# Hymba layer on one Trainium2 core: Toeplitz taps from on-chip tiles, bias tiles built on chip in two halves, and broadcast columns turned by transposes

## The chip, the cores and the metric

One core of a Trainium2 chip runs the whole layer as one launch. The metric is the device time in microseconds (us). The kernel before takes 2327.94 us, the median of three runs (2321.54 to 2329.34 us).

## The reference, cut to what matters

One encoder layer over 2048 frames of width 1024, in float32. One projection gives a state-space input `u` (512 columns: 32 groups of 16) and the queries, keys and values of 8 attention heads of width 64. Both halves are normalised, concatenated, projected and added to the residual; a SwiGLU feed-forward part and a last norm follow.

```python
h = rmsnorm(x, norm_mix_g[l]);  proj = h @ w_in[l]
# state space, per group of 16 channels, 64 complex states
bu = jnp.einsum('bsgh,gph->bsgp', uf, b_bar)
_, states = lax.associative_scan(combine, (a, bu), axis=1)
y = jnp.einsum('bsgp,ghp->bsgh', states, c_mat).real + d_skip * uf
# attention: own 64-frame chunk and the 8 before it
rel = jnp.arange(BAND)[None, :] - LEFT_CHUNKS * CHUNK - jnp.arange(CHUNK)[:, None]
bias = rel_bias[:, jnp.clip(rel, -MAX_REL, MAX_REL) + MAX_REL]
scores = einsum('bnqhd,bnkhd->bhnqk', qc, kb) / math.sqrt(HEAD_DIM) + bias
x = x + concat(rmsnorm(y_ssm), rmsnorm(y_att)) @ w_out[l]
x = x + (silu(h2 @ w_gate[l]) * (h2 @ w_up[l])) @ w_down[l]
```

The bias depends on the distance between query and key alone, so that each row of a bias tile is a window, one element further on, of one row of numbers. The state-space layer is computed in blocks of L = 8 frames: a small Toeplitz matrix of 16x16 taps C·A^k·B (plus D on the diagonal) inside a block, and a scan over blocks.

## The kernel before, in words

Nearly every matmul is split into three (`mm3`, L146): each float32 operand is a rounded part (`hi`) and a rest (`lo`), and hi·hi, hi·lo and lo·hi are added in PSUM. TensorE takes them in program order; a scheduler with priorities has laid the instructions out, and each engine runs its own list in order.

**u phase (`u_phase`).** The 2048 frames are four blocks of 512, in the order 1, 2, 3, 0 (`BLOCKS`). For a block, `prep` loads eight tiles of the transposed input (`xt`, L440, 256 KB each) and four tiles of the input itself (`w<-in_x`, L449, 512 KB each), both issued by SyncE (SP). ScalarE (ACT) makes `hi` from each `xt` (L442) and VectorE (DVE) `lo` (L443); ACT squares the `x` tiles and sums them (L450), and `newton` makes the reciprocal root of four columns on DVE (L104 to L112). A `group` is one 128-row slice of `u`: 24 matmuls into one PSUM bank. `finish` (called after the first group of the next block) spreads the four columns of roots over a 128x512 tile (`spread`, L122, bank `pp`), which ACT copies (`pb`, `rsn`), and DVE multiplies each group by it (`us`), which GpSimd (POOL) writes to DRAM. The `pp` banks are two (`psum2`).

**Prologue of the state space (`ssm_prologue`, a generator).** It advances in steps at places that `u_phase` chooses: `LONG = 1, 3, 2` steps after the first group of the later blocks. DVE makes the scaled inputs `bbr`, `bbi` (the B matrix), the powers `pr`, `pi`, the outputs `v` (four tiles, one for four pairs of groups, DRAM copy `vs`) and the inputs `wt` (four). POOL then makes the high powers `a8` and `sw`. The taps come from reloaded copies: `bbr`, `bbi` go to DRAM `bbs` by four POOL DMAs and come back as `bbg`, `vs` comes back as `vg` and `v`, with real and imaginary parts stacked on 128 partitions; then 32 matmuls of 128x16 weights and 128 columns (`pp<-vg,bbg`, `pp<-v,bbg`) and ACT copies into `kt`, which POOL writes to DRAM (`kts`). At the end `transposes` turns the 32 halves of `wt` for the DRAM tensor `bsts`.

**The first attention unit.** It makes the queries and keys of one pair of heads: two chains of 24 matmuls into the `pf` banks. The prologue's last steps are taken between its groups of six matmuls (`PRO`, L44). After it, copies on ACT and DVE and a DMA make `q2h`, `q2l` and `k2`, and the first scores (`sc`) follow.

**Attention and state space.** A score tile is one PSUM pair (`sc`); DVE adds the bias tile `nb` and takes the row minimum (`s`, L829), ACT takes the exponential, TensorE transposes the result (`pt`, L81), and another matmul with `v` follows (`pj`). The bias tiles of 128x640 are loaded per head, 32 times, from a DRAM table `nbms` (`load_nb`, L800). The table is filled in the u phase from the 768-wide rows `nbs`: one DMA of 1024x640 (2560 KB, DRAM to DRAM, L521) in front of the second prepared block's `xt` loads, and two that put 1e30 into the two corners that a frame may not see (L524). `pv_scale` (L880) spreads reciprocal sums over tiles. The state-space units load `U`, `Bst` (from `bsts`), `Tm` (from `kts`) and `Vm` through SP (L549 in `ssm_unit`) and run between heads, with their scan on POOL (L587 to L621).

**The rest.** Gate and w_out (bank `big`), the gate and up projections (`X`, `Y`) and the down projection (`ps`), which hold most of the time. `rstd_steps` (L141) spreads roots there too.

A spread is the same matmul everywhere: the weights are a column broadcast to 128x128, the moving operand is the identity.

Of the kernel before, what the change touches and what calls it, by code (L numbers as in the profile page):

```python
# [13 lines left out]
ALU = mybir.AluOpType  # L14
AX = mybir.AxisListType

P = 128
# [47 lines left out]
LONG = 1, 3, 2  # L65
# [56 lines left out]
def spread(k, te, pb, o, c):  # L122

    for i in range(4):
        te.matmul(pb[:, i * P : (i + 1) * P], o[:, c + i : c + i + 1].to_broadcast([P, P]), k.ident[:], start=True, stop=True)


def rstd_steps(k, te, psum, pool, tag, sq, n, out, **kw):

    nt = out.shape[-1] // P  # L130
    ps = k.t(psum, *tag, **kw)
    sqs = sq if isinstance(sq, list) else [sq]
    for i in range(nt):
        for m, sq in enumerate(sqs):
            te.matmul(ps[:, i : i + 1], sq[:, i * P : (i + 1) * P], k.ones[:], start=m == 0, stop=m == len(sqs) - 1)
    with k.tc.high_priority():
        o = newton(k, pool, ps[:, :nt], n, nt)
    yield
    pb = k.t(psum, *tag, **kw)
    for i in range(nt):  # L140
        te.matmul(pb[:, i * P : (i + 1) * P], o[:, i : i + 1].to_broadcast([P, P]), k.ident[:], start=True, stop=True)  # L141
    k.nc.scalar.copy(out, pb[:, : nt * P])
    yield
# [13 lines left out]
def ssm_prologue(k, ident, S):  # L157
# [3 lines left out]
    with tc.tile_pool(name="pro", bufs=1) as p:  # L161
# [126 lines left out]
        def transposes(b_, wt):  # L288
            bst = k.t(p, "v" if b_ > 1 else "vg", [P, 9 if b_ > 1 else 8, 2, NS], bufs=2)[:, :8]
# [42 lines left out]
        for g2 in range(2):  # L332
            for c, bt in ((0, bbr), (1, bbi)):
                nc.gpsimd.dma_start(S["bb"][:, g2, c].rearrange("q n m -> n q m"), bt[g2 * NS : (g2 + 1) * NS])
        yield
        wts = []
        for b_ in range(4):
            qs = slice(4 * b_, 4 * b_ + 4)
# [7 lines left out]
            yield  # L346
        for b_ in range(4):
# [3 lines left out]
            wts.append(wt)  # L351
            yield
# [13 lines left out]
        kt = k.t(p, "kt", [CH, 8, P], bufs=2)  # L366
        nc.gpsimd.memset(kt[:], 0.0)
        for b_ in range(4):
            nc.gpsimd.dma_start(S["kt"][:, 8 * b_ : 8 * b_ + 8, 0], kt[:])
        bb = k.t(p, "bbg", [P, NG, CH])  # L370
        nc.sync.dma_start(bb[:], S["bb"].rearrange("q g c n m -> (c n) (q g) m"))
        dm = k.t(p, "cm1", [P, 576])[:CH, : NG * CH].rearrange("c (g m) -> c g m", g=NG)
        V.tensor_tensor(dm, ident[:CH, :CH].unsqueeze(1).to_broadcast([CH, NG, CH]),
                        ddt[:].unsqueeze(2).to_broadcast([CH, NG, CH]), op=ALU.mult)
        vgs = []
        for b_ in range(4):
            vgs.append(k.t(p, "vg", [P, 8, P], bufs=2)[:] if b_ < 2 else k.t(p, "v", [P, 9, P], bufs=2)[:, :8])
            nc.sync.dma_start(vgs[b_], S["v"].rearrange("q g c n m -> (c n) (q g) m")[:, 8 * b_ : 8 * b_ + 8, :P])
        for b_ in range(4):
            gs = slice(8 * b_, 8 * b_ + 8)  # L380
            vg = vgs[b_]
            kt = k.t(p, "kt", [CH, 8, P], bufs=2) if b_ < 2 else k.t(p, ("bc", "small")[b_ - 2], [CH, 8, P])
            if b_ == 0:
                yield
            for g0 in (0, 4):
                ps = k.t(k.pro_psum, "pp", [P, 512])[:].rearrange("p (a b) -> p a b", a=4)
                for g in range(4):
                    k.te.matmul(ps[:CH, g, :], bb[:, 8 * b_ + g0 + g, :], vg[:, g0 + g, :], start=True, stop=True)
                nc.scalar.copy(kt[:, g0 : g0 + 4, :], ps[:CH])
                yield  # L390
            V.tensor_tensor(kt[:, :, :CH], kt[:, :, :CH], dm[:, gs], op=ALU.add)
            nc.gpsimd.dma_start(S["kt"][:, gs, 1], kt[:])
# [4 lines left out]
def u_phase(k, ident, S, aw):  # L397
# [3 lines left out]
    with ExitStack() as cx:  # L401
# [113 lines left out]
        for n in range(1, NSB):  # L515
            last, b = BLOCKS[n - 1 : n + 1]
            prep(b)
            if n == 1:
                corner = k.t(p1, "corner", [64, 64])
                nc.gpsimd.memset(corner[:], 1e30)  # L520
                nc.sync.dma_start(S["nbm"][:], bass.AP(S["nb"].tensor, S["nb"].offset + 1, [[768, H], [1, P], [1, 640]]))  # L521
            if n == 3:
                for m in range(2):
                    corners = nc.sync.dma_start(S["nbm"][:, m * 64 : m * 64 + 64, m * 576 : m * 576 + 64].rearrange("h p c -> p h c"), corner[:].unsqueeze(1).to_broadcast([64, H, 64]))  # L524
                    tc.keep_in_program_order(corners)
# [3 lines left out]
            long(LONG[n - 1])  # L529
            if n == NSB - 1:  # L530
                att = att_phase(k, ident, S, aw, X[b], lambda: ST[b])
                next(att)
                long(1)
            now += [group(b, f, f in pf) for f in (1, 2)]
# [3 lines left out]
        long(7 - sum(LONG))  # L538
    return pro, att

# [122 lines left out]
def att_phase(k, ident, S, aw, x0, roots):  # L663

    tc, nc, io, pfs = k.tc, k.nc, k.io, k.pfs
    with ExitStack() as cx:
# [129 lines left out]
        nbs = {}  # L796

        def load_nb(h):
            nb = k.t(aa, "nb", [P, 640], bufs=2)
            nc.sync.dma_start(nb[:], S["nbm"][h])  # L800
            return nb
# [72 lines left out]
        def pv_scale(st):  # L874
# [4 lines left out]
            for i in range(4):  # L879
                k.ta.matmul(pb[:, i * P : (i + 1) * P], rb[:, i].rearrange("p h d -> p (h d)"), ident[:], start=True, stop=True)  # L880
# [19 lines left out]
        aa = cx.enter_context(tc.tile_pool(name="aa", reuse_waits="tile", bufs=1))  # L900
        sp = tc.alloc_tile_pool(name="ssm", reuse_waits="tile", bufs=1)
# [670 lines left out]
def block_kernel(tc, io, phases="pusamf"):  # L1572
# [3 lines left out]
    with ExitStack() as cx:  # L1576
# [4 lines left out]
        def pp():  # L1581
# [5 lines left out]
            "k": k.t(dram, "ks", [2, H, P, SB]), "nbm": k.t(dram, "nbms", [H, P, 640]), "nb": k.t(dram, "nbs", [H, 768]),  # L1587
# [3 lines left out]
            "bb": k.t(dram, "bbs", [NPR, 2, 2, NS, CH]), "kt": k.t(dram, "kts", [CH, NG, 2, P]),  # L1591
# [17 lines left out]
        with tc.tile_pool(name="powers", bufs=1) as p:  # L1609
            S["a8"] = k.t(p, "a8", [P, 2, NPR, 16])  # L1610
            S["sw"] = k.t(p, "sw", [P, 3, 2, NPR])
            with tc.tile_pool(name="apf", bufs=2, space=bass.MemoryType.PSUM, reuse_waits="tile") as k.pfs:
# [64 lines left out]
```

## Time and profile before

| what | us |
|---|---|
| median of three runs | 2327.94 |
| the profiled execution | 2328.99 |
| its span, first to last instruction | 2327.2 |
| TensorE busy in the span | 2197.0 (94%) |
| u phase, to the first matmul of the attention unit | 0 to 116.8 |
| that unit, with taps | 116.8 to 135.4 |
| first score matmul | 143.24 |
| attention and state space | to about 760 |
| gate and w_out | 760 to 1010 |
| gate and up projections | 1010 to 1865 |
| down projection, last norm | 1865 to 2327 |

Times in the profile are counted from the first instruction of the span; 1.8 us of the profiled execution lie around it. PE is TensorE, SPq an instruction of SyncE that issues a DMA, and a row of the chain of waits reads: start, duration, what it was. Tiles have the program's names, "out<-in". A matmul with float32 operands leaves two records in the trace, a transpose or an `mm3` matmul one.

### The profile page before, as it was taken

How to read it: one execution, taken by the hardware profiler on the slowest of the kernel's cores; microseconds unless marked ns; L12 is line 12 of the kernel's file. 1: busy time of each engine (PE TensorE's matmuls, PEld its weight loads, DVE VectorE, ACT ScalarE, POOL GpSimd, SP SyncE). 2: the span in 40 equal slices, each digit the busy share in tenths (PEclk: the TensorE clock that was granted, in tenths of full speed). 3: DMA queues.
4: the chain of work that ended last, by engine and by line, in shares of the span. 5: the costliest groups of instructions: out<-in, count | busy, mean ns of one | idle time of the engine just before them, and what ended most of it. 6: DMA issues, size and time to landing. Idle time of an engine off the chain costs nothing.

```text
span 2327.2 us, 30433 instructions
## 1 busy us (share of the span) xinstructions
PE 2197.0 (94%) x10712; PEld 1852.3 (80%) x10712; DVE 1545.0 (66%) x2695; ACT 1004.7 (43%) x1655; POOL 349.0 (15%) x814
## 2 busy tenths in 40 slices
PE   8878899999997899999999999999999989999997
PEld 6766688898986688878888887888888878888886
DVE  7746545756545756777776668666756477789766
ACT  4435445555556752253333336333333343353321
POOL 3237545466542000000000000000000000000000
PEclk9989899999998999999999999999999999999998
DMA  8967676775654434763554647555423297465641
GB/s 274 291 221 249 194 209 196 200 221 176 193 153 146 141 105 149 245 198 127 182 180 149 235 160 284 183 198 163 167 90 114 68 338 255 163 216 186 227 158 73
DMA packets 225329, 434.90 MB, mean 187 GB/s; under 512 B 43480, under 2 KB 70152, under 8 KB 218072
## 3 DMA queue, kind: packets, MB, share of 16 engines
q1 hardware_dynamic: 220312, 418.79, 55.0%
q0 software_dynamic: 4864, 14.17, 1.9%
q8 instruction: 84, 1.38, 0.2%
q14 instruction: 69, 0.57, 0.1%
HBM read 292.88 MB, written 132.15 MB: 183 GB/s over the span
## 4 chain that ended last, share of the span: by engine, by line
PE 82%; DMA 6%; DVE 6%; POOL 2%; ACT 2%; issue 1%; SPq 1%; DVEq 0%; ACTq 0%; POOLq 0%
PE X L78 20%; PE ps L78 19%; PE Y L78 10%; PE pf L78 10%; PE big L78 9%; PE W L78 5%; PE pj L78 5%; PE sc L78 2%; PE pt L81 2%; DMA xt<-in_xp 2%; DMA xt<-in_xt 1%; DVE lo L154 1%; SPq L549 1%; DMA nb<-nbms 1%; DMA hd<-wc 0%
## 5 line engine op out<-in xcount | busy, mean ns | idle before, releaser
L78 PE MATMUL X<-hi,c 128*128 128x512 f32 x1408 | 451.3, 391 | 8.5 <-DVE c L154 6.9
L78 PE MATMUL ps<-hd,hd 128*128 128x512 f32 (+1 forms) x1968 | 432.0, 382 | 6.1 <-ACT hd L154 3.7
L78 PEld LDWEIGHTS ps<-hd,hd 128*128 128x128 f32 x1968 | 359.3, 190 | 77.5 <-ACT hd L154 4.6
L78 PEld LDWEIGHTS X<-hi,c 128*128 128x128 f32 x1408 | 265.6, 189 | 65.2 <-DVE c L154 7.8
L78 PE MATMUL X<-lo,c 128*128 128x512 f32 x704 | 274.9, 390 | 0.0
L154 ACT CAST hd<-hd 128x1536 fp32r<-128x1536 f32 (+1 forms) x106 | 147.6, 1393 | 238.1 <-DMA hd<-hq 181.9
L78 PE MATMUL Y<-hi,c 128*128 128x512 f32 x704 | 224.1, 389 | 1.5 <-DVE u L1367 1.5
L154 DVE TENSOR_TENSOR hd<-hd 128x1536 fp32r<-128x1536 f32 (+1 forms) x106 | 174.1, 1645 | 28.8 <-ACT hd L154 28.1
L154 DVE TENSOR_TENSOR c<-S,c 128x512 fp32r<-128x512 f32 x176 | 120.9, 688 | 104.1 <-ACT c L154 104.1
L829 DVE CUSTOM_DVE_ANT_0 s<-sc,nb 128x640 f32<-128x640 f32 (+4 forms) x128 | 94.5, 738 | 110.9 <-PE sc L78 98.7
L1491 DVE TENSOR_TENSOR acc<-acc,ps 128x512 f32<-128x512 f32 x196 | 131.3, 684 | 53.0 <-PE ps L78 48.3
L1363 ACT COPY u<-X 128x512 f32<-128x512 f32 x132 | 77.6, 588 | 204.9 <-PE X L78 204.8
L78 PE MATMUL big<-m,woh 128*128 128x512 f32 x512 | 162.7, 400 | 0.0
L78 PE MATMUL pf<-hi,w 128*128 128x512 f32 x416 | 153.1, 420 | 8.9 <-ACT w L154 4.6
L154 ACT CAST c<-S 128x512 fp32r<-128x512 f32 x176 | 109.5, 622 | 118.3 <-PE Y L78 67.0
L78 PEld LDWEIGHTS Y<-hi,c 128*128 128x128 f32 x704 | 132.1, 188 | 29.3 <-DVE u L1367 1.9
L78 PEld LDWEIGHTS X<-lo,c 128*128 128x128 f32 x704 | 132.8, 189 | 27.7
L154 ACT CAST c<-raw 128x512 fp32r<-128x512 f32 x132 | 82.2, 623 | 149.4 <-PE Y L78 71.2
L78 PE MATMUL Y<-lo,c 128*128 128x512 f32 x352 | 137.0, 389 | 0.0
L832 ACT ACTIVATE s<-s,mn 128x640 f32<-128x640 f32 (+4 forms) x128 | 98.0, 765 | 77.2 <-DVE mn L829 76.5
L848 DVE TENSOR_TENSOR ptl<-pt,pth 128x640 fp32r<-128x640 f32 (+3 forms) x152 | 98.3, 647 | 45.8 <-ACT pth L847 44.1
L847 ACT CAST pth<-pt 128x640 fp32r<-128x640 f32 (+3 forms) x152 | 83.7, 551 | 94.8 <-PE pt L81 89.5
(441 smaller groups left out, 4229.3 us busy)
## 6 DMA issues: line engine op xcount, KB each, us to landing
w<-wss SPq DMA_DIRECT2D x36, 1024.0 KB, 6.7
hq<-g SPq DMA_DIRECT2D x140, 256.0 KB, 2.2
hd<-hq SPq DMA_DIRECT2D x42, 768.0 KB, 4.4
hd<-wc SPq DMA_DIRECT2D x42, 768.0 KB, 6.0
raw<-in_w_gate SPq DMA_DIRECT2D x44, 512.0 KB, 3.7
raw<-in_w_up SPq DMA_DIRECT2D x44, 512.0 KB, 4.1
wc<-px SPq DMA_DIRECT2D x66, 256.0 KB, 3.2
wss<-w SPq DMA_DIRECT2D x12, 1024.0 KB, 6.0
```

Source lines behind the costliest of these rows:

```text
L78: return self.tc.keep_in_program_order(self.tc.nc.tensor.matmul(*a, **b))
L81: return self.tc.keep_in_program_order(self.tc.nc.tensor.transpose(*a, **b))
L154: return nc.scalar.copy(hi, raw), nc.vector.tensor_tensor(lo, raw, f32(hi), op=ALU.subtract)
L549: ins = nc.sync.dma_start(out, in_)
L829: nc.vector.tensor_tensor_reduce(s[:, :nk].rearrange("p (a b) -> p a b", a=nch), ps[:, :nch, :half], hd.nb[:, nk - 1 :: -1].rearrange("p ( ...
L832: nc.scalar.activation(s[:, :nk], s[:, :nk], AF.Exp, bias=mn[:], scale=-1.0, accum_out=sums[sb, pr][:, hh, qp : qp + 1])
L847: nc.scalar.copy(pth[:, a:b, qp, :], pt[:, a:b, :])
L848: nc.vector.tensor_tensor(ptl[:, a:b, qp, :], pt[:, a:b, :], f32(pth[:, a:b, qp, :]), op=ALU.subtract)
L1363: nc.scalar.copy(u[:], ps[:])
L1491: V.tensor_tensor(a, a, ps[:], op=ALU.add)
```

## The change

It has three parts.

1. **Spreads.** In `spread`, `rstd_steps` and `pv_scale` the matmul with the identity becomes `transpose`, the instruction that `pt` uses. The trace shows where: 64 in `pv_scale` (bank `pj`), 40 on `big`, 16 on `pp`, 16 on `ps`, 4 on `pf`, 4 on `X`; 144 in all.
2. **Bias.** `nbms` and its three DMAs are gone. Two tiles `nba`, `nbb` stay on chip for the whole of attention; POOL writes 1e30 into their corners once, and per head two DMAs of 64x576 read the rows from `nbs` itself (`bias_rows`). SP issues two DMAs for each of the 32 heads, not one.
3. **Taps.** The DRAM copy `bbs`, its reload and the four reloads of `vs` are gone. Taps are made from the tiles `v`, `bbr`, `bbi` as they lie: 64 partitions for each of the two groups of a pair, real and imaginary part added in PSUM, 64 matmuls of 64x16 weights and 128 columns where 32 of 128x16 stood. The prologue's steps are the table `LONGS` now: outputs (`VO`), inputs (`WI`) and taps (`TA`) of the four tiles, one entry per step: one step for the second block, one after each of the first three groups of the last two blocks, and one at the end. The transposes of `wt` move up between the groups of the first attention unit, where the taps were.

The core of the diff:

```diff
-LONG = 1, 3, 2
+VO, WI, TA = range(3)
+LONGS = ((VO, 0),), ((VO, 1),), ((TA, 0), (VO, 2)), ((TA, 1), (VO, 3)), ((TA, 2), (WI, 0)), ((TA, 3), (WI, 1)), ((WI, 2),), ((WI, 3),)
...
-        te.matmul(pb[:, i * P : (i + 1) * P], o[:, c + i : c + i + 1].to_broadcast([P, P]), k.ident[:], start=True, stop=True)
+        te.transpose(pb[:, i * P : (i + 1) * P], o[:, c + i : c + i + 1].to_broadcast([P, P]), k.ident[:])
...
+            for q in range(4):
+                for c, bt in enumerate((bbr, bbi)):
+                    for g2, ps in enumerate(pss):
+                        rows = slice(g2 * NS, (g2 + 1) * NS)
+                        k.te.matmul(ps[:CH, q, :], bt[rows, 4 * b_ + q, :], vts[b_][c][rows, q, :L, :].rearrange("p k c -> p (k c)"), start=c == 0, stop=c == 1)
+            for g2, ps in enumerate(pss):
+                nc.scalar.copy(kt[:, g2::2, :], ps[:CH])
...
-                    k.te.matmul(ps[:CH, g, :], bb[:, 8 * b_ + g0 + g, :], vg[:, g0 + g, :], start=True, stop=True)
...
-                nc.sync.dma_start(S["nbm"][:], bass.AP(S["nb"].tensor, S["nb"].offset + 1, [[768, H], [1, P], [1, 640]]))
...
+                bias_corners(k, S["nba"])
+                bias_rows(k, S, 0, S["nba"])
...
+            for f in (1, 2):
+                now.append(group(b, f, f in pf))
+                if n > 1:
+                    long(1)
...
+def bias_rows(k, S, h, nb):
+
+    src = bass.AP(S["nb"].tensor, S["nb"].offset + h * 768 + 65, [[1, 64], [1, 576]])
+    k.nc.sync.dma_start(nb[:64, 64:], src)
+    k.nc.sync.dma_start(nb[64:, :576], src)
+    return nb
```

How the lists of instructions stand. First TensorE in the u phase, in the second group of the block prepared third (block 3). Before, the last matmuls of that group (`ps`, with the operands `hi2x`, `lo2x` and the weights `wuh`, `wul`) are followed by the third group (`pf`):

```order
L78 MATMUL ps_846<-hi2x_713,wuh_129 128x512
L78 MATMUL ps_846<-lo2x_714,wuh_129 128x512
L78 MATMUL ps_846<-hi2x_713,wul_130 128x512
L78 MATMUL pf_871<-raw_704,wuh_129 128x512 x2
L78 MATMUL pf_871<-raw_704,wul_130 128x512
```

Now the taps of the first tile stand between the two, 16 matmuls that change between the two `pp` banks and begin so:

```order
L79 MATMUL ps_820<-hi2x_717,wuh_128 128x512
L79 MATMUL ps_820<-lo2x_718,wuh_128 128x512
L79 MATMUL ps_820<-hi2x_717,wul_129 128x512
L79 MATMUL pp_846<-v_600,bbr_420 16x128
L79 MATMUL pp_847<-v_600,bbr_420 16x128
L79 MATMUL pp_846<-v_600,bbi_421 16x128
L79 MATMUL pp_847<-v_600,bbi_421 16x128
```

The second tile's 16 follow after the third group (banks `pp_909`, `pp_910`), the third's and the fourth's in the next block; the same 64 have left the first attention unit, where 32 stood.

Second, ACT at the end of the u phase. Before, the last copies of the spread roots (`pb`, `rsn`) come after all of the last block's operands, and the taps' copies (`kt`) after the casts of the attention weights:

```order
L476 COPY pb_1028<-pp_1023 128x512
L477 COPY rsn_94<-pb_1028 128x8x64
L154 CAST w_1067<-raw_1068 128x1024
L154 CAST w_1072<-raw_1073 128x1024
L472 COPY rsn_94<-pp_1182 128x512
L154 CAST w_1441<-raw_1442 128x1024
L389 COPY kt_1307<-pp_1336 16x512
L389 COPY kt_1307<-pp_1342 16x512
```

Now the copies of the first two tiles' taps stand right behind the last squares of the last block (`w,ss`), and the roots' copies behind them:

```order
L445 ACTIVATE hi_200_1003<-xt_1033,g_mix_86 128x512
L453 ACTIVATE w_151,ss_1037<-w_151 128x1024 x2
L355 COPY kt_845<-pp_846 16x4x128
L355 COPY kt_845<-pp_847 16x4x128
L355 COPY kt_908<-pp_909 16x4x128
L355 COPY kt_908<-pp_910 16x4x128
L479 COPY pb_1076<-pp_1071 128x512
```

The copies of `kt` have moved from the attention unit up to a place behind the last input load, and ahead of the last-but-one spread's copy.

Third, SP where the second prepared block's loads begin. Before, the table's DMA stands ahead of the `xt` loads of that block and the next:

```order
L449 DMA w_152<-in_x 128x1024 x2
L521 DMA nbms_69<-nbs_70 1024x1x640
L440 DMA xt_715<-in_xp 128x512
L440 DMA xt_719<-in_xp 128x512
L440 DMA xt_723<-in_xp 128x512
```

Now two DMAs of the first head's bias rows stand there:

```order
L452 DMA w_151<-in_x 128x1024 x2
L551 DMA nba_106<-nbs_69 64x576
L552 DMA nba_106<-nbs_69 64x576
L443 DMA xt_719<-in_xp 128x512
L443 DMA xt_723<-in_xp 128x512
```

The place in the queue is the same; the transfer of 2560 KB is replaced by two of 64x576 numbers (147 KB each).

More of the change, by code (lines that the diff above doesn't have):

```diff
@@ L140, in rstd_steps @@
     for i in range(nt):
-        te.matmul(pb[:, i * P : (i + 1) * P], o[:, i : i + 1].to_broadcast([P, P]), k.ident[:], start=True, stop=True)
+        te.transpose(pb[:, i * P : (i + 1) * P], o[:, i : i + 1].to_broadcast([P, P]), k.ident[:])
     k.nc.scalar.copy(out, pb[:, : nt * P])
@@ L351, in ssm_prologue @@
             wts.append(wt)
+        for make in LONGS:
+            for m, b_ in make:
+                (outputs, inputs, taps)[m](b_)
             yield
@@ L364, in ssm_prologue @@
             G.tensor_copy(S["sw"][:, n, 1, :], a8[:, 1, :, e])
[L366 to L387, printed above, removed]
-                    k.te.matmul(ps[:CH, g, :], bb[:, 8 * b_ + g0 + g, :], vg[:, g0 + g, :], start=True, stop=True)
[L389 to L392, printed above, removed]
+        yield
         for b_ in range(4):
@@ L528, in u_phase @@
             finish(last, held)
-            long(LONG[n - 1])
+            long(1)
             if n == NSB - 1:
@@ L532, in u_phase @@
                 next(att)
-                long(1)
-            now += [group(b, f, f in pf) for f in (1, 2)]
+            for f in (1, 2):
+                now.append(group(b, f, f in pf))
+                if n > 1:
+                    long(1)
             sums(b)
```

50 lines of the change are left out of this document (29 added, 21 removed).

## The prediction, as put on record

> **What bounds the kernel now.** I read the page first, then the busy time of TensorE by stage, then the chain of waits where TensorE stands still. The page says that TensorE carries the time:
>
> ```profile
> PE 2197.0 (94%) x10712; PEld 1852.3 (80%) x10712; DVE 1545.0 (66%) x2695; ACT 1004.7 (43%) x1655; POOL 349.0 (15%) x814
> ```
>
> What shortens TensorE's own list counts almost in full, and what is left stands in its idle time. By stages (stretch, its length, busy PE with its instructions, then the other engines, granted clock, DMA share, GB/s):
>
> ```profile
> 147.00:160.00 13.00, 0.00 (x0) 0.00 (x0) 0.78 (x3) 0.47 (x1) 0.00 (x0) 0.67 1.01 329
> 160.00:760.00 600.00, 545.79 (x3255) 487.39 (x3256) 336.44 (x646) 326.42 (x672) 296.96 (x704) 0.95 0.63 189
> 760.00:1010.00 250.00, 239.74 (x1121) 199.98 (x1119) 168.87 (x363) 110.96 (x151) 0.00 (x0) 0.97 0.50 168
> ```
>
> TensorE does nothing from 147 to 160. The chain of waits says why (start, duration, what):
>
> ```profile
> 143.24 0.33 PE sc L78
> 143.57 2.66 PE pf L78 x22
> 146.23 13.31 DMA nb<-nbms
> ...
> 159.69 0.29 DVE s L829
> ...
> 160.13 0.76 PE sc L78 x2
> ```
>
> The first bias tile is issued by SP at 146.23, when the first scores are already there, and lands 13.31 us later; DVE cannot empty the only score bank before, and the second scores wait until 160.13. A second hole is in the u phase. First TensorE's instructions, in brackets what it idled for; then SP's; then the chain:
>
> ```profile
> 59.09 0.39 PE L78 MATMUL ps<-hi,wul 128*128 128x512 f32 x1
> 63.94 1.58 PE L78 MATMUL ps<-raw,wuh 128*128 128x512 f32 x2 [4.46 <-ACT raw L442]
> ...
> 75.84 1.06 PE L78 MATMUL pp<-ident,no 128*128 128x128 f32 x8
> ```
> ```profile
> 36.48 0.80 SPq L521 DMA_DIRECT2D nbms<-nbs  x1
> 37.61 15.93 SPq L440 DMA_DIRECT2D xt<-in_xp  x4
> ```
> ```profile
> 34.68 28.46 DMA xt<-in_xp x2
> 93.25 5.44 PE ps L78 x24
> ```
>
> Behind the table's DMA, four issues of `xt` hold SP for 15.93 us, and the inputs of block 3 come late. Its first group has 24 matmuls; such a group takes 5.44 us when fed (last row). It ends at 75.84, though TensorE was free at about 59.3: 16.5 − 5.4 = 11.1 us lost, 4.5 in the gap and the rest in a slow start.
>
> **The change, part 1: the u phase.** TensorE is then busy without a hole up to 135. The chain at the end of that phase, and the groups on `pp` (duration least/median/most in ns, first and last start):
>
> ```profile
> 115.94 0.89 PE pp L78 x8
> 116.83 4.12 PE pf L78 x18
> 120.95 1.85 PE pp L78 x16
> ```
> ```profile
> L78 PE MATMUL pp<-vg,bbg x32: 272/273/282, 120.9 to 126.0; 128*16 128x128 f32 x32
> L81 PE MATMUL pp<-ident,wt x32: 271/273/330, 135.9 to 142.0; 128*128 128x128 f32 x32
> ```
>
> The attention unit starts at 116.83; call this S. Four edits move it.
>
> *The table's transfer goes.* Two loads of 147 KB take its place, so block 3's inputs come when the others did: −11.1. Below it is bounded by nothing gained, if the DMA engines and not this transfer set the pace.
>
> *Taps come in.* Eight records of 16 make 128 records: the trace has no matmul of 64 rows, the nearest row has 16 records in 1.85 us, 0.116 each, with the same 128 columns. 128 x 0.116 = +14.8 us. Below, 7.4, if the two halves of rows run side by side; above, 128 x 0.273 = 35, if each takes its whole latency. I take 14.8, the row's own rate. The Trainium skill's page "TensorEngine Tiling (Array Packing)", section Tiling Modes, says that tiles of 64 rows execute in parallel, and that a change of mode drains the array; by the first the sum would be 7.4 us lower, and no run shown here decides.
>
> *Spreads shrink.* Four on this path: a spread has 8 records in 0.89 us. As transposes they have 4 records; a transpose costs what a record costs, as the chain shows in the middle of attention:
>
> ```profile
> 519.09 0.55 PE pt L81 x5
> ```
>
> 0.55/5 = 0.11 each. So a spread falls from 0.89 to 0.45: −0.44 each, −1.8 here. Nothing gained is the other bound.
>
> *A new wait.* The second tile's taps need the `pp` banks of the first, and ACT copies those only behind the last squares of the last block's input. Before, those are:
>
> ```profile
> 94.05 1.06 ACT L450 ACTIVATE w<-w 128x1024 f32<-128x1024 f32 x1 [0.89 <-DMA w<-in_x]
> 63.17 1.38 ACT L442 ACTIVATE raw<-xt,g_mix 128x512 fp32r<-128x512 f32 x2 [14.55 <-DMA xt<-in_xp]
> 122.82 1.05 ACT L389 COPY kt<-pp 16x512 f32<-16x512 f32 x2
> ```
>
> Without the table the loads come 11.1 to 14.6 us sooner (TensorE's loss, ACT's wait): the last square at about 81.2, done at 82.5, the bank free half a copy later, at 83.0. TensorE gets there at 59.3 + 0.45 + 3 x 5.44 + 3.7 (first taps) = 79.8. So it waits 3.2; at least 0, and 16 if the loads do not come sooner at all. Behind it in TensorE's queue stands the whole rest of the phase; the roots' copy on ACT is behind the same squares.
>
> S becomes 116.8 − 11.1 + 14.8 − 1.8 + 3.2 = 121.9. The phase as a whole gets 5 us longer: the hole pays for the taps, but not for all.
>
> **Part 2: from S to the second scores.** The chain behind the unit's last matmul:
>
> ```profile
> 135.40 0.75 DVE xt L740 x2
> ...
> 138.88 4.32 DMA lo0x<-lo0x
> ```
>
> Before, the unit takes 135.40 − 116.83 = 18.57 us: four rows of taps (7.4) and 48 `pf` matmuls (11.1). Copies and a DMA follow, 7.84 us to the first scores at 143.24, and the 32 transposes of `wt` fill TensorE meanwhile. Now the taps are gone and these transposes (32 x 0.112 = 3.6) stand inside: 11.1 + 3.6 + 7.84 = S + 22.5 = 144.4. The bias tile has lain on chip since the u phase, so DVE empties the bank at once, and the second scores follow the 2.66 us of `pf` work: 147.5. It was 160.13: **−12.6 us**. Of TensorE's fillers none is left for the 7.84; they cost it nothing, since it waits for the copies. Of the clock:
>
> ```profile
> 143.00:146.00 3.00, 2.76 (x24) 1.00 0.99 253
> ...
> 160.00:162.00 2.00, 1.87 (x9) 0.50 0.50 105
> 162.00:164.00 2.00, 2.00 (x11) 0.50 0.60 156
> 164.00:166.00 2.00, 2.00 (x14) 0.72 0.40 68
> ```
>
> After 13 us of idleness TensorE ran at half its clock for some 4.6 us and lost 2.3. The 4.46 us gap at 59 is followed by such a stretch too, so the 7.84 us without fillers will bring one. I count no gain: 0, at best −2.3.
>
> **Part 3: the other spreads.** Two records become one, 144 instructions in all (16 in part 1):
>
> ```profile
> L78 PE MATMUL pj<-ident,rb x128: 270/275/377, 207.8 to 769.1; 128*128 128x128 f32 x128
> L78 PE MATMUL big<-ident,no x80: 271/275/553, 794.5 to 987.9; 128*128 128x128 f32 x80
> L78 PE MATMUL ps<-ident,no x32: 270/275/582, 2199.0 to 2319.4; 128*128 128x128 f32 x32
> L78 PE MATMUL X<-ident,no x8: 271/275/275, 1088.2 to 1089.0; 128*128 128x128 f32 x8
> ```
>
> In attention 64 x 0.111 = 7.1 us, of which TensorE's share of that stage counts (545.79/600 = 0.91): 6.5. On `big` 40 x 0.111 x 0.96 = 4.3. The other 24 (`ps`, `X`, `pf`): 2.6. Together **−13.4 us**. Least: nothing, if a transpose with a broadcast operand takes as long as the two records; most: −14.2, with every record on the path.
>
> **Part 4: SP.** Each head's bias takes two issues and not one:
>
> ```profile
> 160.81 0.39 SPq L549 DMA_DIRECT2D Bst<-bsts  x1
> ...
> 246.14 3.73 SPq L549 DMA_DIRECT2D Tm<-kts  x8
> ```
>
> 0.47 us each in the last row, 32 more make 15 us of SP's time. Most lies in stretches in which SP has nothing due; where a state-space unit waits for its 8 + 8 loads, as there, the two or three issues in front count. I take +1, between 0 and 5. POOL's DMAs of `bsts` now stand between its powers. The first unit's load of them was issued at 160.81 and first used at about 180 (`pj<-U,Bst`, 179.8 in the next row), 19 us later; the use comes 12.6 us sooner, but so does the load, whose place was behind the bias tile: I take 0.
>
> ```profile
> L78 PE MATMUL pj<-U,Bst x64: 377/379/793, 179.8 to 670.3; 128*128 128x256 f32 x64
> ```
>
> **Sum.** −12.6 − 13.4 + 1 = −25.0. The profiled execution took 2328.99 us (span 2327.2), which makes 2304.0; it lies 1.05 above the median of the runs, 2327.94. The median after: **2303 us**, 1.1% less.
>
> **Rivals.**
>
> *Halves of rows side by side.* The taps cost 7.4: S is 7.4 earlier, less 1 that the bank wait takes back: 2296 to 2297. For it: two groups alternate on separate rows and banks. Against: no such pair in the trace.
>
> *The bank wait is longer.* If the last loads come no sooner, S gains 12.8 more: 2316. For it, while those loads ran the DMA engines were nearly full:
>
> ```profile
> 76.00:117.00 41.00, 41.00 (x195) 34.35 (x194) 36.96 (x79) 17.32 (x29) 12.09 (x21) 1.00 0.97 307
> ```
>
> Against: part of that traffic is the table's and the taps' copies, which go. Halfway: 2309.
>
> *Another transfer takes the bias tile's place.* From 147 to 160 the DMA share was 1.01. `Bst`, `U` or the second bias tile, due when everything is 13 us earlier, may come as late as the first did: 5 to 13 us back, 2308 to 2316.
>
> *The spreads do not shrink.* A transpose as long as two records: without part 3 and the 1.8, 2318.
>
> *Transposes starve the clock: slower.* TensorE's clock falls when it is taken for idle; if transposes do not count as work, each of the 36 places where four stand in a row would be followed by a stretch like 160 to 164.6 that loses 2.3 us. 36 x 2.3 = 83 us: 2386 if all do so; from 11 places on (25/2.3) the kernel is slower than before. Against: the five transposes at 519.09 lie in a stretch of full clock:
>
> ```profile
> 520.00:540.00 20.00, 19.92 (x149) 19.05 (x149) 9.93 (x19) 12.35 (x28) 5.21 (x11) 1.00 0.57 146
> ```
>
> The Trainium skill's page "TensorE: Matmul & The Clock Gate", section Part 4: PE-mode transpose, says that transposes do not count as busy TensorE for the full clock. The row speaks against it where transposes are few among matmuls, and four at a time are fewer still.
>
> *Taps by latency.* 35 us of taps put S 20 us later: 2323, hardly a gain.
>
> **How the numbers follow.** A measurement of this kernel tells about 0.3% (7 us) from no change: faster is below 2321, slower above 2335. My forecast (2298 to 2306, with the clock's and SP's bounds) has 0.50. Halves side by side 0.13 (2291 to 2297, with small waits); the bank wait 0.12 (2306 to 2316); another transfer 0.11 (2308 to 2316); spreads that do not shrink 0.04 (2318); taps by latency 0.04 (2323); a starved clock, or some wait of that size that I don't see, 0.06 (above 2335). Faster: 0.50 + 0.13 + 0.12 + 0.11 + 0.04 = 0.90, less 0.01 for sums of two mishaps: 0.89; same 0.05; slower 0.06. A range from 2292 to 2316 leaves out the last three (0.14) and the outer edges of the others.
>
> **What would show it.** In the changed kernel's profile: the stretch before the second scores has no row `DMA nb`, and these come at about 147; block 3's first group no longer starts late; taps have 128 records at about 0.116 us spacing (0.06 for halves side by side, 0.27 for latency); a wait of TensorE for ACT's `kt` copies of 0 to 5 us near 80; spreads of 4 records in 0.45 us at full clock. A first attention unit later than 130, or a new row `DMA U` or `DMA Bst` of more than 5 us behind the second scores, would make the prediction wrong.

## The result, and the profile after

The changed kernel takes 2301.11 us (median of 4 runs, 2296.80 to 2302.64) against 2327.17 us before (median of 4, 2321.54 to 2329.34): ratio 0.9889, 95% interval 0.9866 to 0.9912, so 25.8 us less, between 20 and 31. The forecast of 2303 was close, and that is in part luck: by stages of the profile the start gained 9 us more than forecast and gate and w_out 4 more, attention 7 and the rest 5 less. The profile shows where.

TensorE's row on the page, 19 us less busy in a span shorter by 26.5:

```profile
PE 2178.3 (95%) x10632; PEld 1833.2 (80%) x10632; DVE 1547.4 (67%) x2695; ACT 1002.2 (44%) x1655; POOL 345.6 (15%) x813
```

TensorE's instructions in the u phase and at the first scores, with what it idled for in brackets:

```profile
57.03 0.62 PE L79 MATMUL ps<-raw,wuh 128*128 128x512 f32 x2
...
62.69 0.60 PE L82 MATMUL pp<-ident,no 128*128 128x128 f32 x4
...
68.70 0.39 PE L79 MATMUL pp<-v,bbr 64*16 64x128 f32 x2
70.68 0.28 PE L79 MATMUL pp<-v,bbr 64*16 64x128 f32 x1 [1.59 <-ACT pb L479]
...
72.53 0.73 PE L79 MATMUL pf<-raw,wuh 128*128 128x512 f32 x2
...
78.21 0.86 PE L79 MATMUL pp<-v,bbr 64*16 64x128 f32 x4
79.41 0.40 PE L79 MATMUL pp<-v,bbi 64*16 64x128 f32 x4 [0.33 <-DVE v L287]
...
81.04 0.73 PE L79 MATMUL pf<-raw,wuh 128*128 128x512 f32 x2
...
92.58 0.39 PE L79 MATMUL pp<-v,bbr 64*16 64x128 f32 x2
93.37 0.28 PE L79 MATMUL pp<-v,bbr 64*16 64x128 f32 x1 [0.40 <-ACT pb L479]
...
95.22 0.50 PE L79 MATMUL ps<-hi,wuh 128*128 128x512 f32 x1
...
113.79 0.60 PE L82 MATMUL pp<-ident,no 128*128 128x128 f32 x4
114.15 0.48 PE L79 MATMUL pf<-hi,w 128*128 128x512 f32 x1
...
133.01 0.32 PE L79 MATMUL sc<-hi2x,hi0x 128*128 128x128 f32 x1 [4.09 <-DVE hi2x L767]
136.10 0.47 PE L79 MATMUL sc<-hi2x,lo0x 128*128 128x128 f32 x1 [2.78 <-DMA lo0x<-lo0x]
...
140.88 0.28 PE L79 MATMUL sc<-hi2x,hi0x 128*128 128x256 f32 x1
```

Block 3's first group runs from 57.03 to 62.69 without a gap (it ended at 75.84). S, the start of the attention unit, is 114.15; before, this view has it at 116.59, and the chain at 116.83. The second scores come at 140.88 and not at 160.13. The wait for the bias tile is gone; what is left before the first scores are the copies of the queries and keys and a DMA (4.09 and 2.78). Of the clock, the stretches around the first scores after the change:

```profile
135.00:140.00 5.00, 3.90 (x18) 3.90 (x19) 0.30 (x2) 0.49 (x2) 3.78 (x14) 0.50 0.99 312
140.00:147.00 7.00, 7.00 (x60) 6.97 (x60) 1.99 (x7) 2.51 (x7) 0.00 (x0) 1.00 1.08 357
147.00:160.00 13.00, 13.00 (x77) 11.44 (x75) 6.29 (x14) 6.01 (x15) 0.00 (x0) 1.00 0.36 78
```

The half clock (0.50) lies at 135 to 140 now, between the first and the second scores and in part on waits.

The first starts of four kinds of matmul cut the span into stages; the groups by tile of the changed kernel (counts, duration least/median/most in ns, first and last start):

```profile
L79 PE MATMUL pj<-U,Bst x64: 377/379/764, 158.3 to 652.5; 128*128 128x256 f32 x64
L79 PE MATMUL big<-gh,wgh x48: 389/389/486, 749.3 to 887.7; 128*128 128x512 f32 x48
L79 PE MATMUL X<-hi,c x1408: 388/389/796, 982.9 to 1837.0; 128*128 128x512 f32 x176
L79 PE MATMUL ps<-hd,hd x1968: 277/389/793, 1838.3 to 2284.8; 128*128 128x512 f32 x178, 128*128 128x256 f32 x19
```

The same cut for every profile of this study (one profiled execution each; us):

| kernel | to first `pj<-U,Bst` | attention | gate, w_out | gate, up | down | span |
|---|---|---|---|---|---|---|
| before | 179.8 | 589.3 | 242.3 | 852.6 | 463.2 | 2327.2 |
| changed | 158.3 | 591.0 | 233.6 | 855.4 | 462.4 | 2300.7 |
| spreads alone | 176.7 | 586.5 | 235.5 | 853.7 | 463.4 | 2315.8 |
| bias alone | 156.9 | 600.7 | 244.1 | 855.7 | 464.3 | 2321.7 |
| taps alone | 168.3 | 584.6 | 241.3 | 855.1 | 464.1 | 2313.4 |
| change without transposes | 159.2 | 594.5 | 242.6 | 858.7 | 463.0 | 2318.0 |
| table in two loads | 177.2 | 593.8 | 239.8 | 853.2 | 463.0 | 2327.0 |
| bias part undone | 162.9 | 585.9 | 236.7 | 852.6 | 463.6 | 2301.7 |
| second half from ACT | 159.9 | 600.2 | 236.8 | 855.7 | 464.5 | 2317.1 |
| taps half by half | 161.0 | 591.6 | 236.1 | 855.1 | 462.4 | 2306.2 |
| attention spreads twice | 156.8 | 599.3 | 235.8 | 855.4 | 461.7 | 2309.0 |
| mix spreads twice | 159.7 | 591.4 | 240.9 | 853.3 | 461.6 | 2306.9 |
| transposes behind unit | 159.3 | 591.5 | 236.3 | 854.3 | 463.0 | 2304.4 |
| one bias half | 157.5 | 586.6 | 236.1 | 853.4 | 462.6 | 2296.2 |

How far single profiles can be trusted is seen in the table: four kernels with the changed kernel's attention (the changed one, taps half by half, mix spreads twice, transposes behind unit) have 591.0 to 591.6 there; the gate and up projections, hardly touched by any edit, vary by 6 us.

The change won 21.5 us up to the first state-space matmul and 8.7 in the gate and w_out stage, and gave back 1.7 in attention and 2.0 behind.

### The profile page after: what moved, and what is told of

Its sections match the earlier page's. It is cut to its first block, busy times and chain, and to the rows that moved or that the text cites. A ratio compares the mean times of both kernels' runs of the same rounds, so it can differ in the third digit from the quotient of the medians.

```text
span 2300.7 us, 30278 instructions
## 1 busy us (share of the span) xinstructions
PE 2178.3 (95%) x10632; PEld 1833.2 (80%) x10632; DVE 1547.4 (67%) x2695; ACT 1002.2 (44%) x1655; POOL 345.6 (15%) x813
## 4 chain that ended last, share of the span: by engine, by line
PE 68%; DVE 5%; ACT 1%; DMA 1%; issue 1%; SPq 0%; DVEq 0%; ACTq 0%
PE X L79 20%; PE ps L79 19%; PE Y L79 10%; PE big L79 9%; PE W L79 5%; PE pf L79 3%; PE pj L79 1%; DVE lo L155 1%; PE sc L79 1%; PE pt L82 1%; DMA lo<-hc 0%; ACT ys L1020 0%; DVE hd L155 0%; DVE u L1381 0%; DVE acc L1551 0%
## 5 line engine op out<-in xcount | busy, mean ns | idle before, releaser
L155 ACT CAST c<-S 128x512 fp32r<-128x512 f32 x176 | 109.5, 622 | 121.6 <-PE Y L79 61.9
L79 PE MATMUL W<-hi,c 128*128 128x512 f32 x352 | 115.5, 389 | 0.0
```

The source lines that it names most:

```text
L79: return self.tc.keep_in_program_order(self.tc.nc.tensor.matmul(*a, **b))
L155: return nc.scalar.copy(hi, raw), nc.vector.tensor_tensor(lo, raw, f32(hi), op=ALU.subtract)
```

## The experiments

Ratios are to runs of the kernel before on the same chip, and differences in us are such a ratio times 2327.17; the times in us of different chips are not compared with each other.

### Each part alone

**Spreads alone**: the kernel before with

```diff
-        te.matmul(pb[...], o[...].to_broadcast([P, P]), k.ident[:], start=True, stop=True)
+        te.transpose(pb[...], o[...].to_broadcast([P, P]), k.ident[:])
```

in the three places.

> The kernel before with only the spreads made transposes. If every record saved counts where TensorE is busy (144 records of 0.111 us, 16.0 us of TensorE; 1.8 of it in the u phase): 12 to 15 us less than before. Rival, that attention's length is set by its loads and the state-space chain and not by TensorE: the 64 records of the bank pj (7.1 us) bring nothing, and the whole is 6 to 9 us less.

Measured: 2316.59 us, ratio 0.9948 (0.9930 to 0.9967), 12.1 us less, between 8 and 16. It lies at the low edge of the first expectation; of the rival's 6 to 9 the interval takes in the upper end alone. By stage: 3.1 at the start, 2.8 in attention, 6.8 in the gate and w_out stage. Attention's share is short of its 7.1.

**Bias alone**: the kernel before with the second part of the diff.

```diff
-                nc.sync.dma_start(S["nbm"][:], bass.AP(S["nb"].tensor, S["nb"].offset + 1, [[768, H], [1, P], [1, 640]]))
+                bias_corners(k, S["nba"])
+                bias_rows(k, S, 0, S["nba"])
```

> The kernel before with only the bias tiles in halves and no table. If the table's transfer made both holes: the late inputs of block 3 (11 us) and the wait for the first bias tile (13 us) both go, about 24 us less, less what comes back. Theory that SP's 32 more issues cost attention little: 20 to 24 us less. Rival, that the issues delay the loads of the state space and of the attention weights by 5 to 9 us in all: 13 to 18 us less.

Measured: 2318.54 us, ratio 0.9961 (0.9946 to 0.9977), 9.1 us less, between 5 and 13. One of the 11 runs took 4447.65 us; the ratio leaves it out. The start is 22.9 us earlier, as the theory has it, and attention 11.4 us longer; the total lies below even the rival's range.

This run also shows what made the hole in the u phase. Block 3's first group ends where the next spread starts, here (first row) and with the taps alone, which keeps the table (second row):

```profile
64.86 1.05 PE L78 MATMUL pp<-ident,no 128*128 128x128 f32 x8
```
```profile
73.33 1.91 PE L79 MATMUL pp<-ident,no 128*128 128x128 f32 x8
```

In the five kernels of the table above that keep `nbms` this point lies at 71.2 to 75.9, in the nine without it at 61.0 to 64.9.

**Taps alone**: the kernel before with `LONGS`, the taps from on-chip tiles and nothing else.

```diff
-LONG = 1, 3, 2
+LONGS = ((VO, 0),), ((VO, 1),), ((TA, 0), (VO, 2)), ((TA, 1), (VO, 3)), ((TA, 2), (WI, 0)), ((TA, 3), (WI, 1)), ((WI, 2),), ((WI, 3),)
```

> The kernel before with only the taps from on-chip tiles, the table and the matmul spreads as they were. Taps in pairs on two halves of the rows take 0.055 us a record, so TensorE has as much to do as before and only at other places: within 4 us of before, the wait for the first bias tile unchanged at about 13 us. If the taps brought a gain of their own (their reloads gone from the loads of the u phase): 4 to 8 us less.

Measured: 2314.55 us, ratio 0.9941 (0.9920 to 0.9962), 13.7 us less, between 9 and 19; a miss by the first expectation and more than the second. SP's list and TensorE's scores show why:

```profile
140.74 0.50 SPq L754 DMA_DIRECT2D hi1x<-hi1x  x1
141.59 0.33 SPq L805 DMA_DIRECT2D nb<-nbms  x1
```
```profile
145.40 0.47 PE L79 MATMUL sc<-hi2x,lo0x 128*128 128x128 f32 x1 [1.89 <-DMA lo0x<-lo0x]
150.85 0.28 PE L79 MATMUL sc<-hi2x,hi0x 128*128 128x256 f32 x1
```

The first bias tile is still loaded from the table, but SP issues it at 141.59, 4.6 us sooner than before, and no instruction waits for it. It was there when DVE made its first tile `s` at 145.92, so it took 4.3 us at most, not 13.31. The second scores follow 5.4 us behind the first, at 150.85. The hole at 147 closes without the bias part.

The three parts alone make 9.1 + 13.7 + 12.1 = 34.9 us, together 25.8: bias and taps close the same hole behind the first scores. At the start they win 22.9 and 11.5 alone, and all three together no more than 21.5.

### All but one part

**Change without transposes**: the changed kernel with the three lines of the spreads as they were.

> The changed kernel with the spreads as matmuls again. All saved records count: 12 to 15 us more than the changed kernel, 2313 to 2316. Attention not bound by TensorE: 6 to 9 us more, 2307 to 2310.

Measured: 2323.83 us (12 runs, 2316.14 to 2333.03), ratio 0.9980 (0.9964 to 0.9997), only 4.7 us less than before, between 1 and 8. Against the changed kernel's 25.8 that would make the transposes worth 21 us, by the ends of the two intervals between 12 and 30. The first expectation, 12 to 15, is at the low end of that, the second is missed. The profiles of the two differ by 17.3: 3.5 in attention, 9.0 in the gate and w_out stage, 3.3 in the gate and up projections, where one spread of four matmuls stands. This kernel's runs spread over 17 us, and the profiled one (2319.80) lies 4 below their median. The 144 records of 0.111 us account for 16 of the 21; the rest stays unexplained.

This kernel has the bias and the taps part, and it gains less than the taps alone (13.7; ratios 0.9980 and 0.9941, with intervals that do not touch). By the profiles the bias part on top of the taps wins 9.1 us at the start and loses 9.9 in attention and 3.6 in the gate and up projections. Why the loss is greater than the gain here is not shown.

**Bias part undone**: the changed kernel with the table and its loads back.

> The changed kernel with the table back: taps and transposes alone. By the parts measured alone, the start (to the first state-space matmul) is about 166, 8 us later than with the change, and attention shorter by 6 to 9, some 582. Theory that the bias part gives back in attention what it gains ahead: within 3 us of the changed kernel, 2299 to 2304. Rival, that it is worth its gain at the start: 7 to 10 us more, 2308 to 2311.

Measured: 2304.68 us, ratio 0.9900 (0.9886 to 0.9915), 23.3 us less than before, beside the change's 25.8 with overlapping intervals. The start is 4.6 us later, attention 5.1 us shorter, both less than expected. The theory holds: in company of the other two, the bias part gives back in attention about what it gains ahead. Taps and spreads alone thus have 23.3 of the 25.8 us, close to the sum of the two alone (13.7 + 12.1); that the bias part adds anything to them is not shown.

### What lengthens attention

**Table in two loads**: the kernel before with

```diff
-            nc.sync.dma_start(nb[:], S["nbm"][h])
+            nc.sync.dma_start(nb[:64], S["nbm"][h, :64])
+            nc.sync.dma_start(nb[64:], S["nbm"][h, 64:])
```

> The kernel before with each head's tile loaded from the table by two DMAs of 64x640, not one of 128x640: the same bytes, 32 more issues for SP. If the issues (and where they push other loads in SP's list) lengthened attention by 11 us with the bias in halves: 7 to 11 us more than before, from more waits for the input tiles and for the state space's loads. If the direct reads from the bias rows did it: within 3 us of before.

Measured: 2333.95 us, ratio 1.0028 (1.0014 to 1.0042), 6.5 us more, between 3 and 10, just below what the issues were expected to cost. Attention is 4.5 us longer in the profile (593.8 against 589.3), which is less than half of the 11.4 of the bias alone; where the other 7 come from, no run shows. TensorE's list is the same as before to the instruction; SP's has 31 rows more, and the scheduler has put loads of input tiles (`xt`), weights (`w`) and state-space tiles (`Bst`, `U`) at other places among them. TensorE's waits in attention, first of the kernel before, then of this one (waited for: us in total, times, longest):

```profile
PE pf L78 <- ACT hi L706: 4.3, 2, 2.3
```
```profile
PE pf L78 <- ACT hi L706: 8.0, 3, 3.1
PE pj L78 <- DMA U<-u: 2.0, 1, 2.0
```

`hi` is made from the `xt` tiles that now come later. The same rows of the changed kernel:

```profile
PE pt L82 <- DVE ptl L860: 13.0, 10, 3.3
PE pj L79 <- DMA Tm<-kts: 8.9, 4, 3.8
...
PE pf L79 <- ACT hi L720: 7.2, 3, 3.1
...
PE pj L79 <- DMA U<-u: 1.7, 1, 1.7
```

In every kernel with two SP issues per head this wait for `hi` takes 7.0 to 9.4 us; in those with one and whole tiles (before, spreads alone, taps alone, bias part undone) 4.0 to 5.4. From the kernel before to the changed one no wait grew more, but that is 2.9 us.

**One bias half**: the changed kernel, which after the first reload leaves the second half of each bias tile as it is (the bias of other heads stays in 64 of its rows).

```diff
-    k.nc.sync.dma_start(nb[64:, :576], src)
+    if both:
+        k.nc.sync.dma_start(nb[64:, :576], src)
```

> The changed kernel, in which every head's reload after the first leaves out the second half of the bias tile (stale numbers stay there): SP has one bias issue per head, as before the change, and half the bytes. If the second issue and what it moves in SP's list cost attention 5 to 7 us, as with the table in two loads: 4 to 7 us less than the change. If not: within 2 us.

Measured: 2298.58 us, ratio 0.9874 (0.9850 to 0.9899), 3.5 us less than the change's own ratio gives, with overlapping intervals. Attention has 586.6 us where four kernels with both halves have 591.0 to 591.6. The wait for `hi` is 6.5 us, between the two groups. With the undone bias (585.9) this puts the price of the second issue, its bytes and the reordering that it brings at about 5 us of attention. Which wait carries it is not shown: against the changed kernel TensorE stands still 1.9 us less (61.9 against 63.7) and is busy 2.6 us less, at a granted clock of 0.96 against 0.95.

**Second half from ACT**: the changed kernel with

```diff
-    k.nc.sync.dma_start(nb[64:, :576], src)
+    k.nc.scalar.dma_start(nb[64:, :576], src)
```

> The changed kernel with the second bias half issued by ScalarE. If SP's issues cost attention its 6 to 9 us: SP has as many as before the change, and the time is 4 to 9 us less, 2292 to 2297. If not the issues: within 3 us of the change; more than that if ScalarE's own list is delayed by them.

Measured: 2316.11 us, ratio 0.9949 (0.9937 to 0.9961), 14 us worse than the change, as the last case had it (more than 3), but its reason doesn't show: no wait of TensorE for ScalarE is longer than in the changed kernel. Its waits in attention:

```profile
PE pj L79 <- DMA Tm<-kts: 16.1, 5, 5.0
...
PE pf L79 <- ACT hi L720: 5.0, 2, 3.1
...
PE pj L79 <- DMA U<-u: 4.4, 1, 4.4
```

The wait for `hi` fell to 5.0, as with one issue, but those for the state space's loads rose by 10 us. SP's list is another one again, and SP's own waits show what made `Tm` and `U` late (L563 issues the state space's loads):

```profile
SPq L563 <- DMA nbb<-nbs: 8.9, 2, 6.3
SPq L563 <- DMA nba<-nbs: 4.2, 1, 4.2
```

Three times in attention SP holds a state-space load until a bias half has landed, 13.1 us in all; in attention of the other kernels it never does. Right behind these three TensorE waits 4.4, 1.3 and 5.0 us for `U` or `Tm`. So not the number of issues alone decides, but which load stands behind which.

### What a tap and a spread cost

**Taps half by half**: the changed kernel with the loops of the taps turned.

```diff
-            for q in range(4):
-                for c, bt in enumerate((bbr, bbi)):
-                    for g2, ps in enumerate(pss):
+            for g2, ps in enumerate(pss):
+                for q in range(4):
+                    for c, bt in enumerate((bbr, bbi)):
```

> The changed kernel with each tile's taps ordered by row half: eight matmuls on partitions 0 to 63, then eight on 64 to 127. If neighbours on different halves run side by side: taps take about 0.11 us a record in place of 0.055, 1.7 us more a tile, and the first attention unit starts up to 7 us later than 114.15; the whole 5 to 7 us more. If a matmul of 64 rows is short by itself: nothing changes.

Measured: ratio 0.9892 (0.9878 to 0.9905), no difference in the whole that can be told from the change's 0.9889. In the trace, the last tile's taps and the next group, first of the changed kernel, then of this one:

```profile
100.91 0.40 PE L79 MATMUL pp<-v,bbr 64*16 64x128 f32 x4
101.13 0.39 PE L79 MATMUL pp<-v,bbi 64*16 64x128 f32 x4
...
102.44 0.39 PE L79 MATMUL pp<-v,bbi 64*16 64x128 f32 x4
102.76 0.50 PE L79 MATMUL ps<-hi,wuh 128*128 128x512 f32 x1
```
```profile
102.39 0.39 PE L79 MATMUL pp<-v,bbr 64*16 64x128 f32 x2
102.62 0.38 PE L79 MATMUL pp<-v,bbi 64*16 64x128 f32 x2
...
103.71 0.40 PE L79 MATMUL pp<-v,bbr 64*16 64x128 f32 x4
103.93 0.40 PE L79 MATMUL pp<-v,bbi 64*16 64x128 f32 x4
...
105.25 0.38 PE L79 MATMUL pp<-v,bbi 64*16 64x128 f32 x2
105.56 0.50 PE L79 MATMUL ps<-hi,wuh 128*128 128x512 f32 x1
```

Four records per 0.22 us where halves alternate, two where they don't, but for the turn from one half to the other, where four of each overlap again (103.71 and 103.93): 32 records and the way to the next group take 1.85 us against 3.17. Neighbours on different halves of the rows run side by side. In these orders the PSUM bank changes with the half; no run separates the two. Of the 5.3 us that four tiles win by it, 3.7 go to waits of the changed kernel that this one doesn't have (below). So the unit starts at 116.95, 2.8 us later than 114.15, and 1.5 of that was there when block 3 began (58.52 against 57.03), ahead of any tap.

**Attention spreads twice**: the changed kernel with

```diff
-            for i in range(4):
+            for i in (0, 1, 2, 3, 0, 1, 2, 3):
                 k.ta.transpose(pb[:, i * P : (i + 1) * P], rb[:, i].rearrange("p h d -> p (h d)"), ident[:])
```

> The changed kernel with each transposed spread of the bank pj done twice: 64 transposes more, 7.1 us of TensorE in attention. If TensorE set attention's length at these places: 6 to 7 us more than the change. If other waits set it: 0 to 3 us more, and the idle time of TensorE in attention falls by the rest.

Measured: ratio 0.9914 (0.9892 to 0.9937), 5.8 us more than the change's ratio gives, with overlapping intervals; attention 599.3 in this profile against 591.0 to 591.6 in the four with the changed kernel's attention, about 8 us more. Added spreads cost attention their whole length.

**Mix spreads twice**: the changed kernel with `spread` called twice in the gate and w_out stage.

```diff
                     spread(k, te, pcs[c], b.o[c], 0)
+                    spread(k, te, pcs[c], b.o[c], 0)
```

> The changed kernel with the transposed spreads of the gate and w_out stage done twice (those called as spread; not those of rstd_steps). If a spread there costs its records: about 0.45 us each, 3 us more for seven of them. If a spread costs more than its records in that stage, as a stage shorter by 6 to 8 us for 40 records suggests: 5 us or more.

Measured: ratio 0.9920 (0.9895 to 0.9945), 7.2 us more than the change's ratio, with overlapping intervals. Of the 32 transposes more, 28 stand on `big`; they lengthen the places where spreads stand there from 4.33 to 7.8 us, 3.5 us, 0.12 each. The stage grew by 7.3 against the changed kernel's profile and by 5 against three others with the same stage (235.8 to 236.3). By its places a spread costs its records; whether the rest is more than the variation of this stage's profiles, this run doesn't decide.

### A next step

**Transposes behind unit**: the changed kernel with `PRO` all zero.

```diff
-PRO = 0, 0, 2, 2, 2, 2, 0, 0, 0
+PRO = 0, 0, 0, 0, 0, 0, 0, 0, 0
```

> The changed kernel with the 32 transposes of wt behind the first attention unit again, not between its groups (PRO all zero). They would fill the 7 us in which TensorE waits for the copies of the queries and keys, and the first scores come 3.6 us sooner: 2 to 4 us less than the change. If the loads of bsts, then later, hold the first state-space matmul: 0 to 3 us more.

Measured: ratio 0.9892 (0.9867 to 0.9918), as the change. The first scores do come sooner, but then:

```profile
130.61 0.27 PE L79 MATMUL sc<-hi2x,lo0x 128*128 128x128 f32 x1
140.25 0.58 PE L79 MATMUL sc<-hi2x,hi0x 128*128 128x256 f32 x1 [6.45 <-DVE mn L841]
```
```profile
139.90 0.29 DVE L841 CUSTOM_DVE_ANT_0 s<-sc,nba 128x128 f32<-128x128 f32 x1 [6.85 <-DMA bsts<-v]
```

The first scores are complete 5.5 us earlier (130.61 against 136.10), and the second come at 140.25 against 140.88. Of both, 2.4 us are not the edit's: the unit itself starts at 111.70 in this profile and not at 114.15. From its start the first scores win 3.0 us, near the 3.6 expected, and the second lose 1.8. DVE's first tile `s` waits for the DMA that writes the transposed `wt` out; POOL issues the two `bsts<-v` from 134.85 on, where the changed kernel had them at 124.75 and 127.87. A new wait took the place of the old one. No version measured beats the changed kernel beyond its interval.

## Why the prediction was right, point by point

*The hole in the u phase: right.* Forecast −11.1. Block 3's first group took 5.66 us where it took 16.5 from the end of the block before: −10.9. The kernels with and without the table (under “Bias alone”) show that its transfer was the cause.

*The taps: mis-sized, and the rival held.* "128 x 0.116 = +14.8 us" was 7.4 without waits: four times 1.85, the fourth tile's time. The halves run side by side. By that rule of the Trainium skill, "TensorEngine Tiling (Array Packing)", section Tiling Modes, the sum was to be 7.4 us lower, and the trace agrees: 1.85 us against 3.17 in the half-by-half order. Half by half the four tiles would have cost 12.7 us (four times 3.17).

*The new wait: about right in size, at another place.* Forecast 3.2 us at the second tile's banks, for the copies of `kt`. TensorE waited 1.59 at the first tile and 0.40 at the third, for the copy of the spread roots (`pb`), and 0.33 at the second for `v`. With what each wait brings, the first three tiles took 3.83, 2.83 and 2.64 us from the first record to the next group, 3.7 more than three times 1.85. That the size fits is luck.

*From S to the second scores: right.* Forecast S + 25.6; it was 140.88 − 114.15 = 26.7. The work between the first and the second scores took 4.8 us (136.10 to 140.88) where the forecast had 3.0, since it stands in the stretch of half clock. But that the bias tile on chip was needed for it was only half the cause: with the taps out of the unit the tile from the table was in time too.

*The clock: counted as 0, and in the end about 0.* Behind the second scores the good end of the range came true: before, 19.7 us passed from them (160.13) to the first state-space matmul (179.8), after, 17.4 (140.88 to 158.3): −2.3. But the new stretch of half clock that the prediction expected ahead of them cost 1.7 us there: the same 24 records and the scores took 3.1 us before (from 143.24) and 4.8 now.

*The spreads: right by the piece, too high in attention.* Two spreads on `big`, before and after, each with the row behind it:

```profile
875.76 1.05 PE L78 MATMUL big<-ident,no 128*128 128x128 f32 x8
876.65 0.95 PE L78 MATMUL big<-ones,sq 128*128 128x1 f32 x8
```
```profile
852.13 0.60 PE L82 MATMUL big<-ident,no 128*128 128x128 f32 x4
852.57 0.95 PE L79 MATMUL big<-ones,sq 128*128 128x1 f32 x8
```

A spread went from 0.89 to 0.43 us (0.45 forecast); the 16 in attention, each from its first record to the next other matmul, took 17.64 us in all before and 11.8 after, waits included, those on `big` 9.39 and 4.33 (−5.1, forecast −4.3). The stage of gate and w_out grew shorter by 6.8 (alone) and 8.7 (in the change; 5.5 to 6.5 in the other kernels that keep its spreads). Attention was to gain 6.5 and gained 2.8 with the spreads alone, 3.5 between the two kernels with all else, and lost 1.3 between taps alone and the undone bias; doubled spreads cost 7.9. Why removed work brings so little there while added work is paid in full is not shown: TensorE's idle time in attention rose from 55.4 to 57.6 us with the spreads alone, but the four kernels with the changed kernel's attention have 58.4 to 64.6 at the same length.

*SP: mis-sized on the other side.* "I take +1, between 0 and 5": the second issue of each head, with the places that other loads then get, cost about 5 us of attention in the change (591.0 against 585.9 and 586.6) and 4.5 in the kernel with the table in two loads. The prediction looked only at loads of the state space; the wait that grew most was that for `hi`, made from the input tiles `xt` of the next block (4.3 to 7.2 us).

*The other rivals did not come.* No transfer took the bias tile's place: TensorE's waits for `U` in attention are 1.7 us in all. The spreads shrank, and the taps took 0.055 us a record and not 0.27.

The sum, by stages of the two profiles: the start gained 21.5 us and not 12.6, for the most part the taps' 7.4 and the 2.3 of clock behind the second scores; attention lost 1.7 where 5.5 were to be gained (spreads and SP); gate and w_out gained 8.7 and not 4.3; the rest lost 2.0 where 2.6 were to be gained, within what these stages vary by. −26.5 in all against −25.0: a taps term 7 us too dear hid that attention brought nothing. No clock starved by transposes: attention has the clock of before (0.95), the gate and w_out stage 0.98 against 0.96. The Trainium skill's sentence that transposes do not count as busy TensorE ("TensorE: Matmul & The Clock Gate", Part 4: PE-mode transpose) showed no effect for four at a time. For longer rows of them it is open: the 32 of `wt`, with 2.0 us of idleness among them, ran at a clock of 1.00 in the kernel before (135.9 to 142.3), but the last 20 at 0.58 with the transposes behind the unit (126 to 130).

## What to carry to other kernels

Price parts of a change together where they touch one hole: bias and taps were worth 9 and 14 us alone and 5 together, since either closed the wait behind the first scores and the bias part lengthens attention. 32 more DMA issues on SP cost attention about 5 us here, and moving them to ScalarE cost the kernel 14 more: look at which loads change places in the queue and what they then wait for, not at the sum of issue times. A right total says little on its parts; the stage table does.

## What the runs showed of the hardware

Matmuls with 64 rows and 128 columns, alternating between partitions 0 to 63 and 64 to 127 and between two PSUM banks, took 0.055 us a record (four in 0.22 us), against 0.11 in the same half and bank (two in 0.22). With the way to the next group, 32 records took 1.85 us in the one order and 3.17 in the other, and 16 records of the 128-row matmuls of before 1.85. A spread directly behind 8 us of idleness, at a granted clock of 0.50, took 1.70 us before and 0.74 after, against 0.89 and 0.43 elsewhere: it saved 0.96 us there and 0.46 elsewhere.
